# The merge with the tokens standing, and modulation weights in buffers of their own

## The chip, the cores and the metric

The kernel runs on one core of a Trainium2 chip. The metric is the device time of one execution in microseconds. Engines are called by their names or as the profile shortens them: TensorE (PE, its weight loads PEld), VectorE (DVE), ScalarE (ACT), GpSimd (POOL) and SyncE (SP), whose queue issues the DMAs in order.

## The reference: one layer of a hybrid diffusion backbone

256 tokens with 2048 channels pass one layer; 256 context tokens give keys, values and recurrence states besides. All is fp32.

```python
def modulate(x, w, shift, scale):
    return rms_norm(x, w) * (1.0 + scale) + shift

def merge_branches(att, rec, gate_a, gate_r, w_branch_attn, w_branch_rec, w_out):
    y = jax.nn.sigmoid(gate_a) * (att @ w_branch_attn) + jax.nn.sigmoid(gate_r) * (rec @ w_branch_rec)
    return y @ w_out

def hybrid_layer(...):
    sh1, sc1, g1, sh2, sc2, g2 = jnp.split(mod[:, None, :], N_MOD, axis=-1)
    h = modulate(x, norm1_w, sh1, sc1)
    hc = modulate(ctx, norm1_w, csh1, csc1)
    ak, av, rff, rfb, ri, aq, rq, rg, gate_a, gate_r = split_cols(h @ w_in, len(IN_SPLITS))
    ...
    att = diff_attn_readout(o_att, subln_w, lam_init)      # 8 heads, two softmaxes each, their difference
    rec = rec_readout(o_f + o_b, rg, rec_gnorm_w)          # 8 heads, gated linear recurrence both ways
    x = x + g1 * merge_branches(att, rec, gate_a, gate_r, w_branch_attn, w_branch_rec, w_out)
    x = x + g2 * conv_ffn(modulate(x, norm2_w, sh2, sc2), w_up, conv_w, conv_b, w_down)

def reference(...):
    mod = jax.nn.silu(c) @ w_mod[l] + b_mod[l]             # 2048 x 12288
    ...
    return rms_norm(x, final_norm_w)
```

## The kernel before

Activations lie with channels on the 128 partitions and tokens along the free axis, `hx[k]` holding 256 latent and 256 context tokens of channel block k. Every fp32 weight is split into a high part and a rest that TensorE multiplies in its faster fp32r form, and every activation likewise. `stage` (line 65) loads one 512 KB unit into the ring `raw` of four buffers, ScalarE casts it to `whi` (line 72), VectorE subtracts to get `wlo` (line 73), each with three buffers. A 128 x 128 block of weights stands in TensorE and tokens move. Where context is wanted, three 512-wide matmuls do a step (`mm3`, lines 77 to 79). For latent tokens alone, `gemm2_unit` (lines 126 and 127) uses a pair: `whi` against high and rest of x side by side (512 wide), `wlo` against the high part (256 wide); `fold` adds the two halves afterwards.

The stages follow each other: start-up (the first two of six modulation vectors, norm, first seven tiles), attention (8 heads), recurrence (8 heads), merge (16 channel blocks j: two gate tiles, a product with each branch, line 703 on; the gates are computed two j ahead), w_out, up product (44 pairs of tiles), down product (16 tiles of six units), final norm.

Beside the weights of the stages run "flows" (generators such as the steps of an attention head) and the modulation's remaining four vectors. `tick` is called once for every weight unit (twice for one of `mm3`), moves the flows on and calls `background` at a rate per stage (`BG_ATT`, `BG_REC`, `BG_MRG`). One background unit (line 336 on) loads 512 KB of w_mod into the same ring `raw`, and one unit later VectorE multiplies it with the conditioning vector `cb` and reduces it in one instruction (line 345). There are 128 such units, the last flushed in w_out at j = 10. `high_priority` in `stage` lets the scheduler put casts and splits ahead of other work of the two engines; otherwise the built order comes from the scheduler and the buffers.

Buffers of the tag `x1` (four of 4 KB a partition) hold first `cb`, then the recurrence's outputs `rraw`, gates, and the residual stream; those of the tag `ar` (16 of 2 KB) hold E and kn in the recurrence, att and rec, and later the normalized h2 of the up product. `acc` is three PSUM banks; `acc5` (tag `m`, four banks) lives from the merge on, in banks which the recurrence's pool `rps` had.

Two places of the recurrence matter below. At h = 0 the steps of head 0 (`ktp` line 565, `dc` 571, seven level products `lv` 590, `op` 598 to 601) stand beside gate tiles for j = 0 and 1 (line 655 in `pre`). Behind the last head come eight rg tiles, `drain`, and the statistic of the recurrence (lines 667 to 672), a Sqrt over all tokens.

## Time and profile before

| | |
|---|---|
| median of 3 runs | 1903.94 us (1903.0 to 1904.11) |
| the profiled execution | 1898.9 us |
| its span, first to last instruction | 1897.1 us |
| mean granted clock of TensorE | 0.996 of full speed |
| busy: TensorE, VectorE, ScalarE, GpSimd | 97%, 71%, 52%, 20% |
| moved by DMA | 385.71 MB, 203 GB/s over the span |

The stages in the profiled execution begin at about 0 (start-up), 145 (attention), 430 (recurrence), 800 (merge), 1057 (w_out), 1147 (up) and 1638 us (down). Times of instructions are from that one execution, so sums are to be held against its 1898.9 us, not against the median. "Idle before" an instruction is time its engine waited, with what released it. A matmul's start is recorded, its end is modelled: the distance from start to start tells what a stream of them costs.

### The profile page before, as it was taken

What the parts mean: (1) busy time and instruction counts of PE and PEld (TensorE: products, weight loads), DVE (VectorE), ACT (ScalarE), POOL (GpSimd) and SP (SyncE); (2) the same over time, 40 slices, a digit from 0 to 9 for tenths busy, and PEclk for the clock granted to TensorE, in tenths of its full rate; (3) what the DMA queues carried; (4) which work ended last, traced back from release to release, by engine and by line L of the source; (5) the groups of instructions that cost most, each with busy time, mean ns of one, the idle gap of its engine ahead of it and who ended that gap; (6) DMA issues with size and microseconds to landing.
All of it is one profiled execution on the core that took longest, in us unless ns stands there. A gap on an engine that the chain in (4) does not pass through costs nothing.

```text
span 1897.1 us, 27964 instructions
## 1 busy us (share of the span) xinstructions
PE 1841.9 (97%) x10430; PEld 1555.5 (82%) x10430; DVE 1354.3 (71%) x2130; ACT 992.7 (52%) x1501; POOL 377.6 (20%) x328
## 2 busy tenths in 40 slices
PE   7999999998999999999999999999999999999997
PEld 3777787777788888888888889888888888888886
DVE  4549878888866677977777879767677677654444
ACT  3336445447655556744444556555555555534442
POOL 0002111103223333401110110322222222211111
PEclk9999999999999999999999999999999999999998
DMA  9977665674333334688888865666666666666664
GB/s 374 370 274 248 202 197 186 207 267 145 97 111 113 110 103 122 210 269 273 280 272 272 276 192 183 192 189 190 190 188 191 188 195 187 185 193 187 192 192 123
DMA packets 112360, 385.71 MB, mean 203 GB/s; under 512 B 12384, under 2 KB 16608, under 8 KB 112224
## 3 DMA queue, kind: packets, MB, share of 16 engines
q1 hardware_dynamic: 112224, 383.92, 63.9%
q8 instruction: 82, 1.34, 0.3%
q14 instruction: 54, 0.44, 0.1%
HBM read 381.78 MB, written 2.10 MB: 202 GB/s over the span
## 4 chain that ended last, share of the span: by engine, by line
PE 72%; DMA 11%; DVE 10%; issue 4%; ACT 2%; POOL 0%; DVEq 0%; SPq 0%; ACTq 0%; POOLq 0%
PE macc L126 28%; PE macc L127 14%; DMA raw<-in_wm 8%; PE acc L126 5%; PE acc L78 4%; PE acc L79 4%; PE acc L77 4%; DVE wlo L73 3%; PE acc L127 3%; PE g L177 2%; DMA raw<-in_win 2%; DVE raw L345 2%; PE acc L177 2%; PE nat L177 2%; ACT whi L72 1%
## 5 line engine op out<-in xcount | busy, mean ns | idle before, releaser
L73 DVE TENSOR_TENSOR wlo<-raw,whi 128x1024 fp32r<-128x1024 f32 (+1 forms) x514 | 626.8, 1220 | 240.2 <-ACT whi L72 234.4
L72 ACT CAST whi<-raw 128x1024 fp32r<-128x1024 f32 (+1 forms) x514 | 530.6, 1033 | 469.9 <-PE macc L126 155.5
L126 PE MATMUL macc<-h,whi 128*128 128x512 f32 x1344 | 466.0, 391 | 0.0
L127 PE MATMUL macc<-h,wlo 128*128 128x256 f32 x1344 | 376.3, 280 | 0.0
L126 PE MATMUL acc<-h,whi 128*128 128x512 f32 x896 | 323.6, 402 | 1.1 <-DVE kkq L143 0.7
L126 PEld LDWEIGHTS macc<-h,whi 128*128 128x128 f32 x1344 | 251.3, 187 | 55.1
L127 PE MATMUL acc<-h,wlo 128*128 128x256 f32 x896 | 254.3, 284 | 6.2 <-DVE wlo L73 5.9
L127 PEld LDWEIGHTS macc<-h,wlo 128*128 128x128 f32 x1344 | 254.0, 189 | 0.0
L126 PE MATMUL macc<-f,whi 128*128 128x512 f32 x704 | 244.1, 391 | 0.0
L77 PE MATMUL acc<-h,whi 128*128 128x512 f32 x528 | 211.8, 401 | 0.0
L345 DVE SCALAR_TENSOR_TENSOR raw<-raw,cb 128x1024 f32<-128x1024 f32 x128 | 162.2, 1270 | 67.0 <-DMA raw<-in_wm 66.5
L78 PE MATMUL acc<-h,whi 128*128 128x512 f32 x528 | 207.0, 392 | 0.0
L79 PE MATMUL acc<-h,wlo 128*128 128x512 f32 x528 | 206.7, 391 | 0.0
L126 PEld LDWEIGHTS acc<-h,whi 128*128 128x128 f32 x896 | 169.1, 189 | 39.7 <-PE acc L127 1.0
L127 PE MATMUL macc<-f,wlo 128*128 128x256 f32 x704 | 197.1, 280 | 0.0
L127 PEld LDWEIGHTS acc<-h,wlo 128*128 128x128 f32 x896 | 170.0, 190 | 12.8 <-DVE wlo L73 12.2
L126 PEld LDWEIGHTS macc<-f,whi 128*128 128x128 f32 x704 | 131.6, 187 | 28.9
L842 POOL TENSOR_TENSOR u<-u 128x256 f32<-128x256 f32 x44 | 69.2, 1572 | 328.0 <-DVE u L837 288.0
L127 PEld LDWEIGHTS macc<-f,wlo 128*128 128x128 f32 x704 | 133.1, 189 | 0.0
L77 PEld LDWEIGHTS acc<-h,whi 128*128 128x128 f32 x528 | 99.2, 188 | 21.9 <-issue 2.9
L79 PEld LDWEIGHTS acc<-h,wlo 128*128 128x128 f32 x528 | 99.1, 188 | 21.5 <-issue 0.6
L78 PEld LDWEIGHTS acc<-h,whi 128*128 128x128 f32 x528 | 99.3, 188 | 20.5 <-issue 1.8
(740 smaller groups left out, 2639.0 us busy)
## 6 DMA issues: line engine op xcount, KB each, us to landing
raw<-in_win SPq DMA_DIRECT2D x178, 512.0 KB, 4.3
raw<-in_wup SPq DMA_DIRECT2D x168, 512.0 KB, 3.6
raw<-in_wm SPq DMA_DIRECT2D x128, 512.0 KB, 4.3
raw<-in_wdn SPq DMA_DIRECT2D x80, 512.0 KB, 3.7
nraw<-in_wn SPq DMA_DIRECT2D x64, 512.0 KB, 7.8
raw<-in_wout SPq DMA_DIRECT2D x32, 512.0 KB, 4.4
raw<-in_wba SPq DMA_DIRECT2D x16, 512.0 KB, 4.5
raw<-in_wbr SPq DMA_DIRECT2D x16, 512.0 KB, 4.7
```

The source lines that it names most:

```text
L72: act.copy(hi[:, :n], raw[:, :n])
L73: dve.tensor_sub(lo[:, :n], raw[:, :n], hi[:, :n].bitcast(F32))
L77: pe.matmul(ps, wh, xh, start=first, stop=False)
L78: pe.matmul(ps, wh, xl, start=False, stop=False)
L79: pe.matmul(ps, wl, xh, start=False, stop=last)
L126: pe.matmul(ps, hi[:, c_], xs[k][:, :, :T], start=k == 0, stop=False)
L127: pe.matmul(ps[:, :T], lo[:, c_], xs[k][:, 0, :T], start=False, stop=k == len(xs) - 1)
L177: tc.keep_in_program_order(pe.matmul(*args, **kw))
L345: dve.scalar_tensor_tensor(raw, raw, 1.0, cb[half], op0=ALU.mult, op1=ALU.mult, accum_out=modp[:, t - 32, half:half + 1])
L842: pool.tensor_tensor(cs[1], cs[0], cs[1], ALU.mult)
```

## The change

**Merge.** `gemmx` makes tokens stand and weights move: for a step of 128 input channels and 512 output channels, each half of the tokens takes three 512-wide matmuls (high x high, rest x high, high x rest), into two PSUM banks. Gate and branch weights are laid out 512 wide on the host (`wgt`, `wbr`). Four groups g of 512 channels replace sixteen j; results have tokens on partitions, so rrstd becomes a column of two values a partition, and the flow `turn` transposes each group back with eight transposes, through `acc` banks, into `y`. gate(0, 0) stands beside head 0 of the recurrence, gate(1, 0) behind the rg tiles, branch_att(0) behind `drain`. Head 0's flow starts its first step five ticks in, not one.

**Modulation.** `x1` has five buffers instead of four. In attention and merge a background unit takes an `x1` buffer, in the recurrence one of the ring as before (`lane`). Reductions wait in `held` until two ticks have passed. 96 units remain for these stages, half of them in the attention, all done before w_out, where sums and residual loads now stand. The last vector (16 tiles) is done as 64 half units of 256 KB in the down product, in `ar` buffers which the up product has released; the conditioning is loaded and computed again for it (`cond`, `cq`). Rates are set anew, NB is 9, the rg temporaries use the one buffer of the tag `sq`, and w_out takes four banks at a time.

```diff
-NB = 10
+NB = 9
-BG_ATT, BG_REC, BG_MRG = 0.7, 0.1, 0.55
+BG_ATT, BG_REC, BG_MRG, BG_DN = 0.63, 0.12, 0.46, 0.35
...
+    held = []
+
+    def background_end(age=0):
+
+        while held and held[0][0] >= age:
+            _, raw, c_, dst = held.pop(0)
+            dve.scalar_tensor_tensor(raw, raw, 1.0, c_, op0=ALU.mult, op1=ALU.mult, accum_out=dst)
 
     def tick(n):
         bg_rate[1] += n * bg_rate[0]
+        for item in held:
+            item[0] += n
+        background_end(2)
...
+    def gemmx(pss, units, xs, k=0):
+
+
+        for src in units:
+            hi, lo = stage(src, 1024)
+            for i in range(2):
+                c_ = slice(i * 512, (i + 1) * 512)
+                for m in range(2):
+                    t_ = slice(m * P, (m + 1) * P)
+                    pe.matmul(pss[m], xs[k][:, 0, t_], hi[:, c_], start=k == 0, stop=False)
+                    pe.matmul(pss[m], xs[k][:, 1, t_], hi[:, c_], start=False, stop=False)
+                for m in range(2):
+                    t_ = slice(m * P, (m + 1) * P)
+                    pe.matmul(pss[m], xs[k][:, 0, t_], lo[:, c_], start=False, stop=k == len(xs) - 1)
+                k += 1
+            tick(1)
...
+    def gate(i, g, accs):
+
+        pss = [accs() for _ in range(2)]
+        gemmx(pss, [wgt_d[i, g, u] for u in range(8)], hx)
+        dst = big.tile([P, 2, 512], F32, tag="x1", name="gate", bufs=5)
+        for m in range(2):
+            act.activation(dst[:, m], pss[m], AF.Sigmoid)
+        return dst
+
+    def branch_att(ga, g, accs):
+        pa = [accs() for _ in range(2)]
+        gemmx(pa, [wbr_d[0, g, u] for u in range(4)], att)
+        for m in range(2):
+            dve.tensor_mul(ga[:, m], pa[m], ga[:, m])
...
-                    raw = stg.tile([P, 1024], F32, tag="raw", name="raw", bufs=4)
+                    if lane[0]:
+                        raw = big.tile([P, 1024], F32, tag="x1", name="bgraw", bufs=5)
+                    else:
+                        raw = stg.tile([P, 1024], F32, tag="raw", name="raw", bufs=4)
                     dma.dma_start(raw, wm_d[t - 32, half])
...
-                yield 1
+                yield 5 if h == 0 else 1
...
-                    pre = [gates(j, g01[:, j]) for j in range(2)]
+                    pre = [gate(0, 0, acc3)]
...
-                t_ = rt.tile([P, T], F32, tag="rg", name="rg")
+                t_ = rt.tile([P, T], F32, tag="sq", name="rg")
...
+            pre.append(gate(1, 0, acc3))
             drain()
+
+            branch_att(pre[0], 0, acc3)
             sp = rps.tile([P, 4, P], F32, tag="aux", name="sp", bufs=2)
...
+            for m in range(2):
+                t_ = slice(m * P, (m + 1) * P)
+                pe.matmul(sp[:, m, 0:2], sqacc[:, t_], ones[:, 0:2], start=True, stop=False)
+                pe.matmul(sp[:, m, 0:2], sqlast[:, t_], ones[:, 0:2], start=False, stop=True)
+            act.activation(rrstd, sp[:, 0:2, 0], AF.Sqrt, bias=epst, scale=1.0 / 1024)
...
+    for g in range(4):
+        ga, gr = pre if g == 0 else [gate(i, g, acc5) for i in range(2)]
+        if g:
+            branch_att(ga, g, acc5)
+        pr = [acc5() for _ in range(2)]
+        gemmx(pr, [wbr_d[1, g, u] for u in range(4)], rec)
+        for m in range(2):
+            dve.scalar_tensor_tensor(gr[:, m], pr[m], rrstd[:, m:m + 1], gr[:, m], op0=ALU.mult, op1=ALU.mult)
+            dve.tensor_add(gr[:, m], gr[:, m], ga[:, m])
+        yy = et.tile([P, 4, 2, T], F32R, tag="y", name=f"y{g}", bufs=4)
+        start(turn(yy, gr))
+        y += [yy[:, i] for i in range(4)]
+    background(len(bg))
+    background_end()
...
+    cq = [big.tile([P, 512], F32, tag="ar", name=f"cq{i}", bufs=16) for i in range(4)]
+    cond(cq, big.tile([P, 512], F32, tag="ar", name="sg", bufs=16), lambda ins: ins)
...
+                raw = big.tile([P, 512], F32, tag="ar", name="bgraw", bufs=16)
+                dma.dma_start(raw, wm_d[48 + t, q // 2, :, (q % 2) * 512:(q % 2 + 1) * 512])
+                held.append([0, raw, cq[q], modq[:, t, q:q + 1]])
+
+    bgf[0] = background_last
+    bg_rate[:] = 2 * BG_DN, 0.0
+    background_last(8)
```

VectorE in the merge, before. `wlo` is the split of a weight unit, line 345 the reduction of a modulation unit, `t` and `gate` the folds and products of a block.

```order
L345 SCALAR_TENSOR_TENSOR raw,modp<-raw,cb_81 128x1024
L73 TENSOR_TENSOR wlo<-raw,whi 128x1024
L143 TENSOR_TENSOR gate<-gate,acc 128x256
L345 SCALAR_TENSOR_TENSOR raw,modp<-raw,cb_81 128x1024
L73 TENSOR_TENSOR wlo<-raw,whi 128x1024 x2
L143 TENSOR_TENSOR gate<-gate,acc 128x256
```

The same engine in the merge, after, in group 1; the reduction is now line 93.

```order
L73 TENSOR_TENSOR wlo_7507<-raw_7504,whi_7506 128x1024
L93 SCALAR_TENSOR_TENSOR bgraw_7502,modp_78<-bgraw_7502,cb1_82 128x1024
L93 SCALAR_TENSOR_TENSOR bgraw_7541,modp_78<-bgraw_7541,cb1_82 128x1024
L73 TENSOR_TENSOR wlo_7525<-raw_7522,whi_7524 128x1024
L73 TENSOR_TENSOR wlo_7546<-raw_7543,whi_7545 128x1024
L93 SCALAR_TENSOR_TENSOR bgraw_7580,modp_78<-bgraw_7580,cb1_82 128x1024
```

The reductions read buffers of their own (`bgraw`), in pairs, and the folds between the splits are gone.

TensorE at the level products of head 0 (`lv`, from the E tiles that ScalarE and VectorE make), before; `acc` is a tile of w_in's product beside it.

```order
L77 MATMUL acc_4129<-h13_1089,whi_4175 128x512
L590 MATMUL lv_3989<-E_3924 128x128 x2
L590 MATMUL lv_4022<-E_3957 128x128 x2
L590 MATMUL lv_4064<-E_3994 128x128 x2
L590 MATMUL lv_4097<-E_4027 128x128 x2
L78 MATMUL acc_4129<-h13_1089,whi_4175 128x512
```

And after, the last of them:

```order
L78 MATMUL acc_3996<-h15_1211,whi_4052 128x512
L79 MATMUL acc_3996<-h15_1211,wlo_4053 128x512
L632 MATMUL lv_4080<-E_4033 128x128 x2
L632 MATMUL lv_4091<-E_4044 128x128 x2
L77 MATMUL acc_4103<-h0_247,whi_4106 128x512
```

Before, four levels stand in a row; now two, with products of the input projection ahead and behind.

VectorE where the down product begins, before; `wlo_15514` is the fifth unit of the first down tile, `wlo_15536` its sixth.

```order
L73 TENSOR_TENSOR wlo_15492<-raw_15489,whi_15491 128x1024
L843 TENSOR_TENSOR sg_15413<-sg_15413,u_15409 128x256
L73 TENSOR_TENSOR wlo_15514<-raw_15511,whi_15513 128x1024
L73 TENSOR_TENSOR wlo_15536<-raw_15533,whi_15535 128x512
L73 TENSOR_TENSOR wlo_15555<-raw_15552,whi_15554 128x1024
```

And after, where `wlo_14828` is the fifth unit and `wlo_14853` the sixth:

```order
L73 TENSOR_TENSOR wlo_14828<-raw_14825,whi_14827 128x1024
L186 TENSOR_TENSOR cq3_14692<-cq3_14692,sg_14693 128x512
L93 SCALAR_TENSOR_TENSOR bgraw_14709,modq_79<-bgraw_14709,cq1_14690 128x512
L93 SCALAR_TENSOR_TENSOR bgraw_14711,modq_79<-bgraw_14711,cq2_14691 128x512
L93 SCALAR_TENSOR_TENSOR bgraw_14713,modq_79<-bgraw_14713,cq3_14692 128x512
L93 SCALAR_TENSOR_TENSOR bgraw_14715,modq_79<-bgraw_14715,cq0_14689 128x512
L93 SCALAR_TENSOR_TENSOR bgraw_14717,modq_79<-bgraw_14717,cq1_14690 128x512
L93 SCALAR_TENSOR_TENSOR bgraw_14719,modq_79<-bgraw_14719,cq2_14691 128x512
L93 SCALAR_TENSOR_TENSOR bgraw_14721,modq_79<-bgraw_14721,cq3_14692 128x512
L93 SCALAR_TENSOR_TENSOR bgraw_14776,modq_79<-bgraw_14776,cq0_14689 128x512
L73 TENSOR_TENSOR wlo_14853<-raw_14850,whi_14852 128x512
```

Nine operations of the last modulation vector stand between the two splits that followed each other.

## Rows read from the trace of the kernel before

**Rows 1.** The page: busy time of the engines; the chain that ended last.
```profile
PE 1841.9 (97%) x10430; PEld 1555.5 (82%) x10430; DVE 1354.3 (71%) x2130; ACT 992.7 (52%) x1501; POOL 377.6 (20%) x328
...
PE 72%; DMA 11%; DVE 10%; issue 4%; ACT 2%; POOL 0%; DVEq 0%; SPq 0%; ACTq 0%; POOLq 0%
PE macc L126 28%; PE macc L127 14%; DMA raw<-in_wm 8%; PE acc L126 5%; PE acc L78 4%; PE acc L79 4%; PE acc L77 4%; DVE wlo L73 3%; PE acc L127 3%; PE g L177 2%; DMA raw<-in_win 2%; DVE raw L345 2%; PE acc L177 2%; PE nat L177 2%; ACT whi L72 1%
```

**Rows 2.** Stretches: length, PE, PEld, DVE, ACT, POOL busy (instructions); clock, DMA share, GB/s.
```profile
145.00:320.00 175.00, 168.85 (x842) 135.46 (x841) 148.89 (x255) 89.38 (x154) 28.73 (x25) 0.99 0.66 210
320.00:440.00 120.00, 113.01 (x584) 92.67 (x583) 97.65 (x163) 62.30 (x104) 8.85 (x13) 1.00 0.71 228
440.00:500.00 60.00, 51.79 (x278) 42.67 (x277) 55.67 (x99) 43.62 (x62) 23.00 (x23) 1.00 0.34 106
...
780.00:800.00 20.00, 18.18 (x104) 15.54 (x104) 19.38 (x39) 14.11 (x27) 5.28 (x4) 1.00 0.78 257
800.00:1057.00 257.00, 251.31 (x1393) 212.87 (x1392) 197.55 (x282) 119.67 (x188) 29.73 (x31) 1.00 0.84 274
...
1638.00:1885.00 247.00, 245.33 (x1414) 215.66 (x1412) 120.29 (x132) 99.81 (x115) 37.53 (x32) 1.00 0.61 177
```

**Rows 3.** Timeline of TensorE: start us, us, what; three places.
```profile
210.09 0.39 PE L79 MATMUL acc<-h,wlo 128*128 128x512 f32 x1
...
211.00 0.39 PE L77 MATMUL acc<-h,whi 128*128 128x512 f32 x1
...
258.39 0.60 PE L425 MATMUL tp<-ident,vr 128*128 128x128 f32 x4
...
259.06 0.28 PE L127 MATMUL acc<-h,wlo 128*128 128x256 f32 x1
...
797.73 0.40 PE L126 MATMUL acc<-h,whi 128*128 128x512 f32 x1
...
802.68 0.40 PE L126 MATMUL acc<-h,whi 128*128 128x512 f32 x1
```

**Rows 4.** Waits in the merge, 780 or 800 to 1057: total us, times, longest.
```profile
PE acc L127 <- DVE wlo L73: 5.1, 12, 1.0
...
SPq L341 <- DVE raw L345: 67.9, 34, 3.7
...
DVE raw L345 <- DMA raw<-in_wm: 32.8, 36, 2.5
```

**Rows 5.** The page's DMA issues: KB each, median us from issue to landing.
```profile
raw<-in_wm SPq DMA_DIRECT2D x128, 512.0 KB, 4.3
```

**Rows 6.** Waits of TensorE from 440 to 500 us.
```profile
PE ktp L565 <- DVE KQ L526: 2.8, 1, 2.8
...
PE lv L590 <- DVE E L552: 1.0, 2, 0.6
```

**Rows 7.** Timeline of ScalarE at the end of the recurrence.
```profile
797.73 1.28 ACT L671 ACT_TABLE_LOAD   x1
799.02 0.48 ACT L671 ACTIVATE rrstd<-sp,epst 128x256 f32<-128x256 f32 x1
```

**Rows 8.** Waits of TensorE in the attention, 145 to 440 us.
```profile
PE S L395 <- ACT p L402: 8.2, 7, 2.2
...
PE acc L127 <- DVE wlo L73: 0.8, 1, 0.8
```

**Rows 9.** Waits of SyncE's queue and of VectorE from 145 to 320 us.
```profile
SPq L68 <- DVE raw L345: 27.9, 13, 4.4
...
DVE raw L345 <- DMA raw<-in_wm: 12.1, 7, 4.5
DVE wlo L73 <- ACT whi L72: 8.1, 6, 3.1
```

**Rows 10.** VectorE by line and shape: busy us, mean ns; idle before, releaser.
```profile
L345 DVE SCALAR_TENSOR_TENSOR raw<-raw,cb 128x1024 f32<-128x1024 f32 x128 | 162.2, 1270 | 67.0 <-DMA raw<-in_wm 66.5
...
L408 DVE SCALAR_TENSOR_TENSOR p<-p,z 128x512 f32<-128x512 f32 x16 | 11.9, 745 | 0.0
```

More of the change, by code (lines that the diff above doesn't have):

```diff
@@ L146, in body, with cond @@
     modv = cpool.tile([P, 96], F32, name="modv")
-    modp = cpool.tile([P, 64, 2], F32, name="modp")
+    modp = cpool.tile([P, 48, 2], F32, name="modp")
+    modq = cpool.tile([P, 16, 4], F32, name="modq")
     sel = cpool.tile([P, 2], F32, name="sel")
-    cb = [big.tile([P, 1024], F32, tag="x1", name=f"cb{i}", bufs=4) for i in range(2)]
+    cb = [big.tile([P, 1024], F32, tag="x1", name=f"cb{i}", bufs=5) for i in range(2)]
+    def cond(parts, sg, pin):
+        n = D // len(parts)
+        for i, part in enumerate(parts):
+            dma.dma_start(part, cb_d[:, i * n:(i + 1) * n])
+            pin(act.activation(sg, part, AF.Sigmoid))
+            pin(dve.tensor_mul(part, part, sg))
     hx = [None] * KT
@@ L294, in body @@
             g0raw[GROUP0[i]] = r
-        sg = big.tile([P, 1024], F32, tag="x1", name="sg", bufs=4)
-        for i in range(2):
-            dma.dma_start(cb[i], cb_d[:, i * 1024:(i + 1) * 1024])
-            tc.keep_in_program_order(act.activation(sg, cb[i], AF.Sigmoid))
-            tc.keep_in_program_order(dve.tensor_mul(cb[i], cb[i], sg))
+        cond(cb, big.tile([P, 1024], F32, tag="x1", name="sg", bufs=5), tc.keep_in_program_order)
     def in_units(t):
@@ L320, in in_tile_early, with acc3 @@
         g0raw[t] = r
-    def gates(j, dst):
-        for i, base in enumerate((GA, GR)):
-            ps = in_tile(base + j)
-            fold(dst[:, i], ps)
-            act.activation(dst[:, i], dst[:, i], AF.Sigmoid)
-        return [dst[:, 0], dst[:, 1]]
-    bg = [(t, half) for half in range(2) for t in range(32, 96)]
+    def acc3():
+        return acc.tile([P, 512], F32, tag="acc", name="acc")
+    def gate(i, g, accs):
[10 more added lines that the diff above has]
+            dve.tensor_mul(ga[:, m], pa[m], ga[:, m])
+    bg = [(t, half) for half in range(2) for t in range(32, 80)]
     with ExitStack() as esa:
-        bg_rate[0] = BG_ATT
-        held = []
+        bg_rate[0] = BG_ATT0
+        lane = [True]
         def background(n):
@@ L483, in body @@
             drain()
-        rraw = [big.tile([P, 4, T], F32, tag="x1", name=f"rraw{i}", bufs=4) for i in range(2)]
-        rrstd = cpool.tile([P, T], F32, name="rrstd")
+        rraw = [big.tile([P, 4, T], F32, tag="x1", name=f"rraw{i}", bufs=5) for i in range(2)]
+        rrstd = cpool.tile([P, 2], F32, name="rrstd")
         with ExitStack() as es:
@@ L611, in head @@
                     pool.tensor_tensor(sqacc, sqacc, sq, ALU.add)
-            background(max(0, len(bg) - 64))
-            g01 = big.tile([P, 2, 2, T], F32, tag="x1", name="g01", bufs=4)
+            background(max(0, len(bg) - 48))
+            background_end()
+            lane[0] = False
             depth[0] = 1
@@ L690, in residual_load @@
     def residual_load(i):
-        t_ = big.tile([P, 4, T], F32, tag="x1", name=f"x1_{i}", bufs=4)
+        t_ = big.tile([P, 4, T], F32, tag="x1", name=f"x1_{i}", bufs=5)
         dma.dma_start(t_, xT_d[:, 4 * i:4 * i + 4])
@@ L725, in body @@
+    background(len(bg))
+    background_end()
+    bg_rate[0] = 0.0
+    mod_sum(32, 80)
+    w2 = cpool.tile([P, KT], F32, name="w2")
+    dve.scalar_tensor_tensor(w2, modv[:, 64:80], 1.0, col("n2w", 0, 16), op0=ALU.add, op1=ALU.mult)
+    for i in range(4):
+        residual_load(i)
     warm = et.tile([P, 1], F32, name="warm")
@@ L767, in body @@
     for j in range(KT):
-        if j % 2 == 0:
-            pair = [(acc5(), [(wout_d[j + i, 0], 1024), (wout_d[j + i, 1], 1024)]) for i in range(2)]
+        if j % 4 == 0:
+            four = [(acc5(), [(wout_d[j + i, 0], 1024), (wout_d[j + i, 1], 1024)]) for i in range(4)]
             if j == 0:
-                gemm2(pair, y)
-        if j > 1:
-            gemm2([pair[j % 2]], y)
-        ps = pair[j % 2][0]
-        sq = residual(j, ps, 32, sqs)
-        if j == 10:
-            background(1000)
-            residual_load(3)
-            mod_sum(48, 96)
-            w2 = cpool.tile([P, KT], F32, name="w2")
-            dve.scalar_tensor_tensor(w2, modv[:, 64:80], 1.0, col("n2w", 0, 16), op0=ALU.add, op1=ALU.mult)
+                gemm2(four, y)
+                drain()
+        if j > 3:
+            gemm2([four[j % 4]], y)
+        ps = four[j % 4][0]
+        sq = residual(j, ps, 32, sqs)
         if j >= 10:
@@ L848, in body @@
         else:
-            fj = et.tile([P, 2, T], F32R, tag="y", name=f"f{j}", bufs=16)
+            if j % 4 == 0:
+                fp = et.tile([P, 4, 2, T], F32R, tag="y", name=f"f{j}", bufs=4)
+            fj = fp[:, j % 4]
         act.copy(fj[:, 0], sg)
```

82 lines of the change are left out of this document (37 added, 45 removed).

## The prediction

> **What bounds the kernel now.** I read the page's busy line and chain first: TensorE is busy 97% of the span, and the chain that ended last is 72% TensorE, 11% DMA, 10% VectorE, the largest DMA piece being `raw<-in_wm`, the modulation weights [rows 1]. So time can leave in two ways: TensorE does less, or its remaining waits get shorter. The table by stretch says where those waits are [rows 2]. The down product (1638 to 1885) holds 1414 matmuls, 707 pairs of a 512-wide and a 256-wide one, in 247 us: 349 ns a pair, with VectorE busy under half the time. That is the stage without stalls. The attention (two rows, 145 to 440) is idle 6.2 and 7.0 us, the start of the recurrence (440 to 500) 8.2 us, its last 20 us 1.8 us, the merge (800 to 1057) 5.7 us. In the merge idle time shows only part of the loss: a late matmul is recorded as a long one, so I go by the pitch.
>
> The pitch from start to start [rows 3]: four 512-wide matmuls from 210.09 to 211.00 us, 0.2275 each. In the merge's gates 14 pairs from 797.73 to 802.68, 353.6 ns a pair. Four transposes with the slow matmul behind them, 258.39 to 259.06 us, less an ordinary 0.235: 0.435 us, 109 ns each.
>
> **The merge's matmuls.** The change computes gates and branches with the tokens standing. Before: 32 gate tiles x 16 = 512 pairs at 353.6 ns (181.0 us) and 32 branch tiles x 8 = 256 pairs at 349 ns, the down product's row, since these too read x without a gap (89.4): 270.4 us. After: 8 gate passes of 16 steps and 8 branch passes of 8 make 192 steps of six 512-wide matmuls, 1152 x 0.2275 = 262.1 us, and 32 transposes x 0.109 = 3.5 us. Net **-4.8 us**. All of it is on the path, as TensorE is the bound. (The folds go too, but VectorE and ScalarE work beside TensorE.) The bound on the other side is pairs at 349 throughout, the lowest pitch shown: 268.0 against 265.6, -2.4.
>
> The Trainium skill speaks against this gain: "TensorE: Matmul & The Clock Gate", Back-to-back issue gap, gives an isolated gap of N/2.4 + 2.5 ns, 216 and 109 ns, and by it eight matmuls (4 x 216 + 4 x 109 = 1300 ns) cost what six do (1296), so that only the transposes would be left, +2.7 us, and the whole sum 7.5 us later. The rows disagree: 228 ns instead of 216, and 350 or more a pair instead of 325; I go by the rows.
>
> **The merge's stalls.** Between 800 and 1057 us lie 1393 matmuls, 448 gate pairs and some 248 branch pairs: 158.4 + 86.8 = 245.2 us at their pitch, so 11.8 us are stalls. The waits tell why [rows 4]: TensorE waits for the low half of the weights (`wlo`); SyncE, issuing in order, stands 67.9 us, 34 times, ahead of a modulation load that waits for a buffer which VectorE has to free by its reduction, and weight loads stand behind; VectorE waits 32.8 us for the modulation data to land, with `wlo` splits queued behind. One ring of four buffers carries both streams. A load lands 4.3 us after its issue (median) [rows 5]; a unit lasts 8 x 0.35 = 2.8 us, and at 0.55 modulation units a tick four buffers are 2.6 weight units, 7.2 us of lead, of which the splits take part. After, the weights own the ring (4 x 2.73 = 10.9 us), the modulation has buffers of its own, and the built order stands reductions at least two units behind their loads. DMA stays the same size, some 192 GB/s of weights and 0.46 units a tick more, about 280 GB/s, what the row of the stretch shows (274 at a share of 0.84). I leave 2 us of stalls: **-9.8 us**, with 0 and -11.8 as bounds.
>
> **Start of the recurrence.** The 8.2 us of idle time are shared [rows 6]: the first `ktp` waits 2.8 us for VectorE's KQ, then level products of head 0 wait for E, and shorter waits follow. In the changed order the first `ktp` has the same cover since head 0's q product (135 and 138 512-wide matmuls, by my count of the order), so its 2.8 us mostly stay, though VectorE and ScalarE lose the folds of four gate tiles. Behind it the levels get 78 matmuls of cover where 45 stood: the row of four level products without anything between is gone. I take **-5 us** (the short waits, and small gaps that the idle time doesn't count), with 0 and -8.2 as bounds.
>
> **End of the recurrence.** gate(1,0) and branch_att(0), 96 + 48 matmuls, move in front of the end, so they cover `op` of head 7. But the four small matmuls for rrstd are followed directly by a product into a PSUM bank which the recurrence's own banks cover, and it waits for the Sqrt that reads them: in the rows of before a cast of some 1 us may stand ahead, then a table load of 1.28 us, then the Sqrt of 0.48 [rows 7]; some 2.3 us of TensorE. Also the rg temporaries now share one buffer, so eight folds wait for POOL one after the other. Against that stands the 1.8 us idle in 780 to 800. I take **0**, from -2 to +4. The Trainium skill puts a drain of about 1.38 us beside each table load ("ScalarE: Activation LUTs", What ACT_TABLE_LOAD costs); here the Sqrt starts 1.29 us after its load did, so no run shows one in this place, and it would add to the end of my range alone.
>
> **Attention.** Modulation loads leave the weights' ring here too. SyncE waited 27.9 us in 13 times with a weight load for a modulation buffer [rows 9]. But the new buffers are free earlier, and the order packs 48 reductions before the 32nd weight unit where 36 stood: 12 x 1.27 us [rows 10] = 15.2 us more for VectorE, which in 145 to 320 is busy 148.9 of 175. None follow until the recurrence, where before 28 did: some 35 us less in the second part. TensorE waits there mainly for the softmax (`S` for `p`, 8.2 us in 7 times [rows 8]), whose steps stand in VectorE's queue. I expect the second part to give back half of its 7.0 us idle and the first to stay: **-3 us**. Bounds: -10 (three quarters of all 13.2 us) and +8 (VectorE's 164 busy plus its present waits for data and for casts, 12.1 and 8.1 [rows 9], exceed 175 by 9).
>
> **Up to down.** The last gate's 64 half units, in the h2 buffers, start when the up product releases these. SyncE issues 4 conditioning loads and 11 half units, each waiting for TensorE, in front of the sixth load of the first down tile; VectorE does one product and eight 512-wide reductions between the fifth and sixth `wlo`, 9 x 0.8 us (a 512-wide operation of the same kind took 745 ns [rows 10], with an accumulator read) = 7.2 us. Three split buffers give a split two units, 5.6 us, less about 2.4 for cast and split, 3.2 us of slack: a stall of 7.2 - 3.2 = **+4 us**, from 0 (it was cast early) to +8 (DMA late as well). Later tiles: four reductions add 3.3 us to some 7.5 of VectorE's 15.4 a tile; no stall.
>
> **Nothing** for w_out with four banks (covered by its own 349 ns pairs), NB = 9 (start-up loads; if that cover fails up to +3), or the residual loads, which now go out before w_out.
>
> Sum against the profiled run, 1898.9 us: -4.8 - 9.8 - 5 + 0 - 3 + 4 = -18.6, 1880.3. The median of the three runs is 1903.94, 5.0 above it, so I add 5.0: **1885.3**, say 1885.
>
> **The rivals.** (A) More comes free: attention gives 10 instead of 3, and the end of the recurrence its 2: 1876, or down to 1869 with the start at its bound. For it: VectorE is what these waits end on, and it loses work there. Against: one S bank stays. (B) The first part of the attention becomes VectorE's: +8 instead of -3 and the later parts as forecast, 1896; with the landing waits of 12 us unmoved up to 1905, near no change. For it: 94% busy. (C) The merge's stalls are the DMA's rate, not the shared ring: share 0.84 before, the same bytes after; then 1885 + 9.8 = 1895. Against it: SyncE's and VectorE's waits name the buffer. The change would then do what it says and be worth half. (D) Slower: in-order SyncE in the attention. Three of the five buffers are free for modulation loads (the conditioning keeps two), and every load behind a busy one holds the weight loads back. 48 units in 170 us is one per 3.5 us, so a buffer's round must stay under 10.6 us: 4.3 to land, 1.3 to reduce, 5.0 in VectorE's queue. If rounds take 13 us, 16 of them are 38 us late, and the weights' lead, four units of some 5 us less landing, cast and split, absorbs about 13: +25, 1910. It decides from a queue wait of some 7 us. Before, SyncE already waited, at most 4.4 us at a time on these [rows 9], yet TensorE lost 0.8 us to `wlo` [rows 8]; so a small chance.
>
> **How the numbers follow.** Forecast (1874 to 1897) 0.58, A 0.14, B 0.10, C 0.10, D 0.08. A measurement of this kernel can tell about 0.2%, 3.8 us, from no change, so "same" is 1900.1 to 1907.7. Faster: 0.57 of the forecast, A, 0.02 to 0.03 of B, most of C, less a reserve for what I haven't seen: 0.79. Same: the upper part of B and a little of C and D: 0.10. Slower: D and the reserve: 0.11. The range leaves out the lower edge of A and D with the top of B: 1869 to 1901.
>
> **What would show it.** Right: merge passes at 0.2275 us a matmul with nearly no `acc <- wlo` waits, SyncE's wait for modulation buffers gone from weight loads; no `lv` waits at head 0; a TensorE gap near 2 us before the first rec product and near 4 us in the first down tile. Wrong: `wlo` waits in the merge at a DMA share near 0.85 (C), VectorE over 95% busy and `wlo` waits in 145 to 320 (B), SyncE waiting long for `bgraw` there (D), or the granted clock at its 1.2 GHz level behind one of the new gaps.

## The result: slower, by 0.7%

The changed kernel takes 1915.24 us (median of 4 runs, 1914.17 to 1917.5) against 1903.47 us before: a ratio of 1.0067 (95% interval 1.0054 to 1.0080). The forecast of 1885 us and its range of 1869 to 1901 us are missed on the wrong side of no change. Two executions taken beside the experiments, one of e1 at 6478 us and one of the kernel before at 4767 us, are left out of every median and ratio below.

The profiled execution has a span of 1915.7 us against 1897.1, 18.6 us more than before (the medians differ by 11.8). Here are the page's busy line and the head of its chain, which answer to [rows 1].

```profile
PE 1844.7 (96%) x10082; PEld 1548.3 (81%) x10082; DVE 1345.9 (70%) x2148; ACT 982.5 (51%) x1423; POOL 342.5 (18%) x296
...
PE 74%; DVE 14%; ACT 4%; issue 3%; DMA 3%; POOL 2%; SPq 0%; DVEq 0%; ACTq 0%; POOLq 0%
```

TensorE has 348 matmuls fewer and is busy for 3 us longer. On the chain DMA fell from 11% to 3%, as meant, while VectorE rose from 10% to 14%, and TensorE, ScalarE and GpSimd by 2 points each: what DMA gave up, the engines took.

To see where, I added up from the starts of all matmuls in the trace how far each lies behind the one ahead of it, less what its shape costs in an undisturbed stream (227, 117 and 112 ns for 512, 256 and 128 columns), and counted what is over 60 ns. In that loss both waits and a slow clock are contained. Times are those of each kernel's own trace; "e" columns are experiments below.

| stretch, us | before | after | e1 | e3 | e5 | e8 |
|---|---|---|---|---|---|---|
| 160 to 440, attention | 28.0 | 19.9 | 19.9 | 29.4 | 29.5 | 19.4 |
| 440 to 520, heads 0 and 1 | 12.6 | 16.9 | 17.9 | 16.1 | 14.3 | 17.9 |
| 520 to 760, later heads | 8.6 | 21.2 | 7.8 | 21.8 | 21.8 | 7.4 |
| 760 to 840, end of recurrence | 5.1 | 6.8 | 9.7 | 8.4 | 11.5 | 4.0 |
| 840 to 1080, merge | 13.8 | 7.6 | 2.7 | 6.0 | 13.9 | 2.6 |
| 1600 to 1880, down product | 0 | 14.6 | 15.7 | 19.1 | 0 | 0 |
| whole execution | 104.5 | 123.1 | 110.4 | 137.1 | 132.4 | 89.9 |

So the change did what the forecast hoped for in the attention (8 us) and the merge (6 us), and lost 17 us in the recurrence and 15 in the down product, besides 2 at the recurrence's end. The whole rows differ by 18.6 us, as the spans do; savings and losses under 60 ns a matmul (the merge has fewer, w_out and the down product a slower stream, see e9) cancel.

The stretches, to be read as [rows 2] (length; PE, PEld, DVE, ACT, POOL busy and instructions; clock, DMA share, GB/s):

```profile
145.00:320.00 175.00, 167.34 (x843) 134.18 (x843) 162.12 (x282) 88.57 (x156) 28.49 (x24) 1.00 0.71 242
320.00:440.00 120.00, 119.79 (x599) 98.41 (x598) 75.83 (x120) 68.26 (x104) 9.10 (x13) 1.00 0.41 126
...
520.00:760.00 240.00, 229.43 (x1186) 195.74 (x1185) 166.69 (x308) 135.97 (x184) 71.26 (x71) 0.99 0.34 105
...
1640.00:1880.00 240.00, 229.59 (x1288) 197.86 (x1287) 157.93 (x283) 94.38 (x109) 39.74 (x29) 0.99 0.78 248
```

The second part of the attention is idle for 0.2 us of 120 where it was 7.0. Between 520 and 760 us TensorE is now idle for 10.6 us; before, the same row had none:

```profile
520.00:760.00 240.00, 240.00 (x1255) 205.49 (x1254) 170.17 (x322) 138.59 (x194) 78.55 (x76) 1.00 0.37 112
```

**The recurrence.** TensorE's waits from 440 to 820 us in the changed kernel (total, times, longest), which answer to [rows 6]:

```profile
PE lv L632 <- DVE E L594: 15.1, 5, 6.9
PE ktp L607 <- issue: 2.7, 1, 2.7
PE lv L632 <- DVE S L635: 1.9, 1, 1.9
```

VectorE around one of the five, in order of start (start, duration), and the matmul that waited for it:

```profile
551.41 0.43 DVE L593 TENSOR_TENSOR E<-E,kkq 128x256 f32<-128x256 f32 x1 [0.72 <-ACT E L591]
551.75 0.69 DVE L686 TENSOR_TENSOR_SCAN PL<-ones,fq 128x256 f32<-128x256 f32 x1
552.35 1.22 DVE L73 TENSOR_TENSOR wlo<-raw,whi 128x1024 fp32r<-128x1024 f32 x1
553.49 1.26 DVE L686 TENSOR_TENSOR_SCAN PL<-ones,fq 128x256 f32<-128x256 f32 x2
554.67 1.25 DVE L688 TENSOR_TENSOR_SCAN PC<-ones,fq 128x256 f32<-128x256 f32 x2
555.84 0.88 DVE L635 COPY_PREDICATED S<-masks,lv 128x128 f32<-128x128 uint32 x4
556.62 0.42 DVE L594 TENSOR_TENSOR E<-E,kkq 128x256 f32<-128x256 f32 x1
...
557.18 0.68 PE L632 MATMUL lv<-E 128*128 128x128 f32 x4 [2.10 <-DVE E L594]
```

A level's E is multiplied in two halves. The first (line 593) starts at 551.4 us; the second (line 594) stands behind the next head's five scans, a split and four masked copies, and starts 5.2 us later. The level product needs both. Counted in the trace by the order of the level products, the five waits stand one each at heads 1, 2, 4, 5 and 6, and the 1.9 us for `S` at head 3. Head 0 has none, where before it had three of up to 1.0 us.

**The down product.** Waits of TensorE and of VectorE from 1640 to 1880 us:

```profile
PE macc L137 <- DVE wlo L73: 10.4, 10, 2.3
...
DVE bgraw L93 <- DMA bgraw<-in_wm: 23.6, 16, 3.7
```

The timeline of VectorE in one such place (start, duration; idle before, releaser):

```profile
1753.27 1.22 DVE L73 TENSOR_TENSOR wlo<-raw,whi 128x1024 fp32r<-128x1024 f32 x1
1758.16 0.69 DVE L93 SCALAR_TENSOR_TENSOR bgraw<-bgraw,cq 128x512 f32<-128x512 f32 x1 [3.67 <-DMA bgraw<-in_wm]
1758.78 0.08 DVE L93 DVE_READ_ACCUMULATOR bgraw<-bgraw,cq 128x1 f32 x1
1758.90 0.16 DVE L931 TENSOR_REDUCE modv<-modq 128x1 f32<-128x4 f32 x1
1758.97 0.68 DVE L93 SCALAR_TENSOR_TENSOR bgraw<-bgraw,cq 128x512 f32<-128x512 f32 x1
1759.58 0.08 DVE L93 DVE_READ_ACCUMULATOR bgraw<-bgraw,cq 128x1 f32 x1
1759.58 1.22 DVE L73 TENSOR_TENSOR wlo<-raw,whi 128x1024 fp32r<-128x1024 f32 x1
```

VectorE stands for 3.7 us at the head of its queue with a reduction whose half unit has not landed; the split that TensorE needs comes behind two reductions. By the trace the reductions stand in the first nine tiles, 12, 6 and 5 in the first three, 8 in each of the next five and 1 in the ninth, where the rate in the code says four a tile.

**The clock.** It differs too. In stretches of 3.4 us TensorE ran at the lower of its two levels, 1.2 GHz: once in mid-kernel before (226.7 us), six times after, one of them 6.8 us long. Three of them (the last column but two is the clock as a share of full speed):

```profile
447.60:451.00 3.40, 3.40 (x16) 3.30 (x16) 2.77 (x8) 1.62 (x2) 0.14 (x1) 0.50 0.18 74
502.20:509.00 6.80, 3.94 (x16) 3.69 (x16) 6.20 (x13) 2.21 (x4) 3.94 (x5) 0.50 0.09 38
...
1761.70:1765.10 3.40, 3.40 (x13) 2.92 (x12) 3.40 (x7) 0.42 (x2) 1.11 (x2) 0.50 0.75 215
```

Each of the six lies behind or partly within a wait of TensorE (of the three shown: 2.7 us for `ktp`, 6.9 for `lv`, 2.3 for the split). Together they are 23.9 us at half speed against 3.4 before, so up to 10 of the 18.6 us (half of the 20.5 us more) are this second price of the waits. The prediction priced none of its waits with it.

### The profile page after: what moved, and what is told of

Read it like the earlier page. It is cut to its first block, busy times and chain, and to the rows that moved or that the text cites. A ratio compares the mean times of both kernels' runs of the same rounds, so it can differ in the third digit from the quotient of the medians.

```text
span 1915.7 us, 27159 instructions
## 1 busy us (share of the span) xinstructions
PE 1844.7 (96%) x10082; PEld 1548.3 (81%) x10082; DVE 1345.9 (70%) x2148; ACT 982.5 (51%) x1423; POOL 342.5 (18%) x296
## 4 chain that ended last, share of the span: by engine, by line
PE 74%; DVE 14%; ACT 4%; issue 3%; DMA 3%; POOL 2%; SPq 0%; DVEq 0%; ACTq 0%; POOLq 0%
PE macc L136 24%; PE macc L137 13%; DVE wlo L73 4%; PE macc L160 4%; PE macc L161 4%; PE macc L164 4%; PE acc L77 3%; PE acc L78 3%; PE acc L79 3%; DVE bgraw L93 3%; PE acc L136 3%; DMA bgraw<-in_wm 2%; PE g L214 2%; PE acc L214 2%; PE nat L214 2%
## 5 line engine op out<-in xcount | busy, mean ns | idle before, releaser
L136 PE MATMUL macc<-f,whi 128*128 128x512 f32 x704 | 248.9, 398 | 0.0
L77 PE MATMUL acc<-h,whi 128*128 128x512 f32 x528 | 212.1, 402 | 0.0
L78 PE MATMUL acc<-h,whi 128*128 128x512 f32 x528 | 206.7, 391 | 0.0
L136 PE MATMUL acc<-h,whi 128*128 128x512 f32 x384 | 141.8, 409 | 0.0
L799 POOL TENSOR_TENSOR sqs<-sqs,sq 128x256 f32<-128x256 f32 x28 | 34.0, 1216 | 507.0 <-ACT sq L798 507.0
L77 PEld LDWEIGHTS acc<-h,whi 128*128 128x128 f32 x528 | 99.7, 189 | 23.4 <-issue 4.6
L79 PEld LDWEIGHTS acc<-h,wlo 128*128 128x128 f32 x528 | 99.3, 188 | 21.0
L78 PEld LDWEIGHTS acc<-h,whi 128*128 128x128 f32 x528 | 99.5, 188 | 18.7 <-issue 0.4
L137 PE MATMUL acc<-h,wlo 128*128 128x256 f32 x384 | 108.5, 283 | 0.0
L93 DVE SCALAR_TENSOR_TENSOR bgraw<-bgraw,cb 128x1024 f32<-128x1024 f32 x81 | 98.9, 1230 | 11.2 <-DMA bgraw<-in_wm 11.2
L136 PE MATMUL macc<-y,whi 128*128 128x512 f32 x256 | 90.7, 399 | 0.0
```

The costliest lines, as they stand in the source:

```text
L77: pe.matmul(ps, wh, xh, start=first, stop=False)
L78: pe.matmul(ps, wh, xl, start=False, stop=False)
L79: pe.matmul(ps, wl, xh, start=False, stop=last)
L93: dve.scalar_tensor_tensor(raw, raw, 1.0, c_, op0=ALU.mult, op1=ALU.mult, accum_out=dst)
L136: pe.matmul(ps, hi[:, c_], xs[k][:, :, :T], start=k == 0, stop=False)
L137: pe.matmul(ps[:, :T], lo[:, c_], xs[k][:, 0, :T], start=False, stop=k == len(xs) - 1)
```

## The experiments

My theory (A) after this reading: the 5 ticks moved every head against the next head's gate arithmetic; in the down product VectorE stands with reductions for late data; buffers of their own helped attention and merge. The rivals are in each expectation.

### e1: the 5 ticks put back to 1

```diff
-                yield 5 if h == 0 else 1
+                yield 1
```

> The changed kernel with one number put back: head 0 of the recurrence takes its first step after 1 tick, not 5. Theory A: the 5 ticks shift every head's steps against the next head's gate arithmetic, so that VectorE's E product of a level stands behind a split, five scans and four masked copies; TensorE's loss beyond its pitch between 440 and 760 us is 38 us in the changed kernel against 21 before. Then this run loses the 2.1 us lv waits of each head and gains 12 to 17 us: 1898 to 1903. Rival: the loss comes with gate(0,0), whose 512-wide results and sigmoids stand beside head 0, or from the modulation; then the lv waits stay and the time stays near 1915.

Measured: 1903.37 us (median of nine runs), 1.0010 of before (0.9997 to 1.0022), 11.9 us less than the changed kernel's median. Between 520 and 760 us no wait of TensorE is left:

```profile
520.00:760.00 240.00, 240.00 (x1263) 205.85 (x1262) 170.66 (x327) 135.77 (x187) 84.81 (x76) 1.00 0.38 118
```

The loss there falls from 21.2 to 7.8 us. The gain lies at the lower edge of the 12 to 17 us expected; in this trace the end of the recurrence loses 2.9 us more. The first heads stay bad (17.9 us): that is not the ticks.

### e5: the 5 ticks alone, in the kernel before

```diff
-                yield 1
+                yield 5 if h == 0 else 1
```

> The kernel before with one number of the change alone: head 0 of the recurrence takes its first step after 5 ticks instead of 1. Theory A: this alone makes each later head lose some 2 us at a level product; TensorE's loss between 520 and 760 us rises from 8.6 to about 20 us, the clock falls in one or two more places, and the kernel is 8 to 15 us slower than before, 1.004 to 1.008 of it. Rival: the 5 ticks only hurt together with gate(0,0) and the new modulation lanes; then it is within 0.2% of before.

Measured: 1921.49 us, 1.0102 of before (1.0079 to 1.0125), 18.8 us slower. One number, without the new merge or a new buffer, costs more than the whole change does, and more than the 8 to 15 us expected. Of what this trace loses more than before, 13 us lie in the later heads, 6 at the end of the recurrence and 5 in w_out, behind a wait of 2.4 us for `y`. The waits of TensorE from 520 to 760 us in this kernel:

```profile
PE lv L590 <- DVE E L552: 9.8, 4, 3.0
```

Before, the same row had no wait. It is the wait of the changed kernel, for the same second half (line 552 here). The rival, that it hurts only beside gate(0,0), falls.

### e2: no last modulation vector in the down product

```diff
-    bgl = [(t, q) for t in range(16) for q in range(4)]
+    bgl = []
+    dve.memset(modq, 0.0)
```

> The changed kernel without the loads and reductions of the last modulation vector in the down product (that vector is left out of the result, its sums are zero). Theory A: these cost the down product 14.6 us of TensorE time beyond its pitch, so 1915 falls to about 1899 to 1901 and every down tile takes 15.25 us. Rival: the slower pitch of the later down tiles (15.55 us instead of 15.25) and the longer down product come from elsewhere (the up product's new buffers, the clock); then less than 8 us return.

Measured: 1899.41 us, 0.9985 of before (0.9973 to 0.9996), 15.8 us less than the changed kernel. The down product is as before, without a wait:

```profile
1640.00:1880.00 240.00, 240.00 (x1387) 211.63 (x1386) 120.03 (x131) 99.69 (x115) 37.27 (x31) 1.00 0.62 182
```

1387 matmuls in 240 us, where the changed kernel did 1288.

### e4: the 64 reductions without their loads

```diff
-                raw = big.tile([P, 512], F32, tag="ar", name="bgraw", bufs=16)
-                dma.dma_start(raw, wm_d[48 + t, q // 2, :, (q % 2) * 512:(q % 2 + 1) * 512])
-                held.append([0, raw, cq[q], modq[:, t, q:q + 1]])
+                held.append([0, one[0], one[1], modq[:, t, q:q + 1]])
```

> The changed kernel with the 64 reductions of the last vector in the down product, on two constant tiles, without their 64 loads (the last vector is wrong). Theory A: TensorE's stalls there come from reductions that wait for late loads at the head of VectorE's in-order queue, splits behind them; without loads under 4 us of stalls remain of 14.6: about 1903. Rival: VectorE's added work by itself makes the splits late; then the stalls stay, 1911 to 1917, since here up to eleven reductions stand in a tile.

Measured: 1899.97 us, 0.9990 of before (0.9976 to 1.0004), 0.6 us from the run without the vector. Waits of TensorE in the down product, and the row of that stretch:

```profile
PE macc L137 <- DVE wlo L73: 0.9, 3, 0.5
```

```profile
1640.00:1880.00 240.00, 239.00 (x1368) 208.88 (x1368) 162.12 (x285) 97.64 (x112) 38.60 (x31) 1.00 0.61 180
```

VectorE is as busy as in the changed kernel (162 against 158 us of 240) and TensorE hardly waits. So it is not VectorE's work but its standing still for data, or the loads by some other way; the next run bears on which.

### e6: the loads at their planned rate

DMA issues of the down product are kept in program order from the second tile on.

```diff
+        if j == 1:
+            pin[0] = tc.keep_in_program_order
...
-        dma.dma_start(raw[:, :n], src)
+        pin[0](dma.dma_start(raw[:, :n], src))
...
-                dma.dma_start(raw, wm_d[48 + t, q // 2, :, (q % 2) * 512:(q % 2 + 1) * 512])
+                pin[0](dma.dma_start(raw, wm_d[48 + t, q // 2, :, (q % 2) * 512:(q % 2 + 1) * 512]))
```

> The changed kernel with the DMA issues of the down product kept in program order from its second tile on, so that the half units of the last vector come at the planned rate, 4 a tile over 13 tiles, not 7 to 8 a tile in the first nine; same loads, same reductions. Theory A: the late landings behind which VectorE stands come from two streams that together ask for 295 GB/s; spread out (some 255 GB/s) most of the 10 us behind the first tile return, the first tile's 4 us stay: 1904 to 1908. Rival: a reduction right behind its load waits whatever the rate; then 1912 to 1917.

Measured: 1912.49 us, 1.0054 of before (1.0037 to 1.0070): 2.8 us better than the changed kernel, not the 7 to 11 expected. My theory's figure falls, the rival's holds. The waits in the down product:

```profile
DVE bgraw L95 <- DMA bgraw<-in_wm: 56.8, 34, 4.4
...
PE macc L139 <- DVE wlo L75: 9.8, 9, 2.6
```

From the third tile on four or five units are reduced a tile, where the changed kernel has up to eight, yet VectorE waits longer (56.8 us, 34 times) and TensorE as long. Behind the first two tiles, which lose 3.0 us more here, this run loses 8.5 us, the changed kernel 10.7. So the rate of the two streams explains little: a reduction that the built order puts shortly behind its load waits for the landing at either rate, and the split behind it is late. No run holds the reductions back longer, which would test this directly.

### e3: the modulation in the weights' ring again

```diff
-                    if lane[0]:
+                    if False:
```

> The changed kernel with the modulation units of all stages in the ring of the weights, as before; the new merge, the last vector in the down product and the 5 ticks stay. Theory A: buffers of their own gave the merge 6 us and the attention 8 us back, so this run is 10 to 14 us slower than the changed kernel, 1925 to 1929, with splits late in the merge. Rival: the tokens standing (no folds, fewer loads of standing operands) gave them, and the ring matters little: 1913 to 1918.

Measured: 1925.35 us, 1.0114 of before (1.0089 to 1.0138), some 10 us slower than the changed kernel, as expected. But the place is not as expected: the attention loses all that it had gained (29.4 us against 19.9, before 28.0), the down product 4.5 more, and the merge nothing (6.0 against 7.6). SyncE does wait in the merge of this run for the shared buffers, with weight loads behind it, and TensorE's splits are in time. From 840 to 1056 us:

```profile
PE macc L164 <- DVE wlo L73: 0.4, 1, 0.4
...
SPq L387 <- DVE raw L93: 42.3, 18, 3.5
SPq L68 <- DVE raw L93: 30.6, 14, 4.7
```

So it is not the ring by itself that the merge's stalls of before went with. What else changed there is the new product, which spares folds (VectorE is busy 143 us of 214 in this run's merge against 166 of 216 before), and the modulation's lower rate: 32 reductions stand in this run's merge, 41 in those 216 us before, at a DMA share of 0.79 against 0.85. Which of these it was, no run separates, and so rival C's cause, the rate of DMA, isn't excluded for the stalls of before.

### e7: 5 ticks to 1, the last vector in the up product

32 whole units, in buffers of the tag `h` which are free there, at 0.4 a tick from tile 4 of the up product on.

```diff
-                yield 5 if h == 0 else 1
+                yield 1
...
+        if j == 4:
+            cq = [big.tile([P, 1024], F32, tag="h", name=f"cq{i}", bufs=16) for i in range(2)]
+            cond(cq, big.tile([P, 1024], F32, tag="h", name="sg", bufs=16), lambda ins: ins)
+            bgf[0] = background_last
+            bg_rate[:] = BG_UP, 0.0
```

> The changed kernel with 1 tick instead of 5 at head 0, and the last modulation vector as 32 whole units in the up product, in buffers of its h tag that are free there, instead of the down product. Theory A: up has no stalls, DMA at 190 GB/s and VectorE at 73%, so it hides 32 units at 0.4 a tick; both losses are gone and the gains stay: 1885 to 1892, faster than before. Rival: the up product takes over the stalls (VectorE above 85% there, loads late), 1897 or more.

Measured: 1899.49 us, 0.9965 of before (0.9940 to 0.9990), but ten runs in two groups: three from 1885.0 to 1888.6, seven from 1898.6 to 1902.1. The three lie in the expected range, the seven where the rival put them, but the stalls of the rival are absent: in the profiled execution, one of the seven, TensorE waits for a split once, 0.4 us. Neither the expectation nor its rival has two groups.

### e8: the same, with rg's own buffer

```diff
-                t_ = rt.tile([P, T], F32, tag="sq", name="rg")
+                t_ = rt.tile([P, T], F32, tag="rg", name="rg")
```

> As the run with the last vector in the up product, with the rg temporaries in a buffer of their own again instead of the shared one of the tag sq. Theory A: the waits of TensorE for rg's fold (3.5 us in the run with 1 tick) go: 2 to 4 us faster than that run. Rival: another wait of the end of the recurrence takes their place, no difference.

Measured: 1894.32 us (five runs, 1892.1 to 1895.2), 0.9955 of before (0.9940 to 0.9970). The end of the recurrence loses 4.0 us where e1 lost 9.7 (e7, without the buffer, 9.5), somewhat more than the expected 2 to 4 us: in e1's trace the waits for rg's fold are 3.5 us with a slow stretch of the clock behind them (792.6 us), and in e8's both are absent. This is a reading of traces; the times alone can't show it, given e7's two groups. TensorE's whole loss is 89.9 us, 14.6 under before, yet the profiled span is only 7.0 under it.

### e9: a different stream of matmuls in between

So 7.6 us are missing in e8, and some 12 if the merge's matmuls spare the 4.8 us forecast. They are mainly in the pitch. In the up and down products of e8, nearly without waits, a pair takes 353 ns, where before it took 347. Does an interruption change it back?

```diff
+    def stir(w, x):
+        d_ = acc.tile([P, 512], F32, tag="acc", name="stir")
+        for i in range(12):
+            pe.matmul(d_[:, :T], w[:, 0, :P], x[:, 0, :T], start=i == 0, stop=i == 11)
...
+        if j in (24, 32):
+            stir(h2[0], h2[1])
...
+    stir(ff[0], ff[1])
```

> The kernel with the last vector in up and its own rg buffer, plus three groups of twelve 256-wide matmuls into a bank that nobody reads: two in the up product (tiles 24 and 32), one ahead of the down product. Theory M: pairs of matmuls run at one of two steady pitches, 347 or 353 ns, and an interruption of the stream decides which; in that kernel up and down run at 353 from 1247 us on. If a different stream of matmuls is such an interruption, the pitch falls back to 347 behind one of the groups, and the 4.2 us that they cost are repaid with up to 10: 1886 to 1890. Rival: the pitch follows from where operands or results lie in memory; then it stays 353, and the time is 4 us longer, 1898.

Measured: 1897.83 us, 0.9976 of before (0.9964 to 0.9987). The pitch stays at 353 behind all three groups, and the groups themselves run at 120 ns a matmul, not 117. A different stream is no interruption in this sense. The time is what the rival expected; its reason, the place of operands and results, doesn't fit e11 below, where the same program holds the other pitch.

### e10 and e11: the same without the last vector, and e8 once more

e10 has 1 tick, rg's own buffer, and the edit of e2; against e8 it lacks the last vector. e11 is the kernel of e8, unchanged.

```diff
-    bgl = [(t, q) for t in range(16) for q in range(4)]
+    bgl = []
+    dve.memset(modq, 0.0)
```

> The changed kernel with 1 tick at head 0, rg in its own buffer, and no last modulation vector at all (its sums are zero and the result lacks it). It differs from the run with the last vector in up by those 32 units alone. Theory M: the units there cost no wait (TensorE lost 1 us beyond its pitch in that up product) but put the stream of up and down on the 353 ns pitch; without them both stay at 347, which for 1376 pairs from 1247 us on and the down product's 704 is 12 us less: about 1880 to 1884. Rival: the slow pitch comes from the new layout or from the chip; then up and down stay at 353 here too, and the time is 1892 to 1895.

> The kernel with the last vector in the up product and rg in its own buffer once more, on this chip beside the run without the last vector. If the pitch is a state that an execution falls into and not a property of the program, its executions spread over some 12 us (1882 to 1896), as they did with the shared rg buffer (1885 to 1902); if it is a property of the program, they lie within 4 us of 1894.

Measured: e10 takes 1882.40 us (1880.5 to 1884.1), 0.9889 of before (0.9869 to 0.9908). e11's ten runs spread from 1879.6 to 1898.2 us with a median of 1894.01, 0.9935 of before (0.9912 to 0.9957). Its profiled execution, of 1879.6 us, has a span of 1877.6 us against 1890.1 in e8, and the same program's loss is the same: 89.5 and 89.9 us. Forty microseconds of the up product, in the kernel before, in e8, in e11 and in e10, as rows of stretches:

```profile
1240.00:1280.00 40.00, 40.00 (x233) 35.28 (x232) 28.64 (x41) 22.72 (x36) 11.63 (x8) 1.00 0.64 192
```

```profile
1240.00:1280.00 40.00, 40.00 (x229) 34.71 (x228) 35.05 (x53) 23.71 (x38) 10.08 (x7) 1.00 0.78 277
```

```profile
1240.00:1280.00 40.00, 40.00 (x233) 35.18 (x232) 35.01 (x54) 24.28 (x38) 9.39 (x7) 1.00 0.79 275
```

```profile
1240.00:1280.00 40.00, 40.00 (x233) 35.27 (x232) 27.98 (x40) 24.06 (x38) 10.67 (x8) 1.00 0.59 186
```

233, 229, 233 and 233 matmuls in 40 us without an idle moment, at the same granted clock and, in e8 and e11, with the same instructions. So the pitch is a state that an execution falls into. The two traces come from different chips, but the ten runs of e11, on one chip, spread over 18.6 us, so the chip alone doesn't decide it. e10's four runs without the units lie close together, and its trace holds 347 ns through up and down; the trace of e11 shows that the units don't force 353. Whether they make it likelier is open. With 12.5 us the pitch is as large as the effect of the whole change.

At the pitch of before, e11's span is 19.5 us under before and its loss 15.0: the other 4.5 us are close to the 4.8 that the merge's matmuls were forecast to spare.

## Why the prediction was wrong, point by point

**The step that failed first** was in "Start of the recurrence". It costed the 5 ticks by the cover they give to head 0, where I read two kernels' orders, and the seven heads behind it at nothing. Flows run one after the other there, so a delay of the first moves them all, and what a head's steps meet in VectorE's queue changes with it. Expected -5 us for the stage; measured +4.3 in heads 0 and 1, +12.6 in the later ones, and by itself, in the kernel before, 18.8 us (e5). At head 0 the sign came as forecast, no `lv` waits: the mechanism held where I looked and failed in the heads behind. In the trace of the changed kernel the pattern repeats with each head.

The row of 2.8 us in [rows 6] I also read for the wrong head. It belongs to head 1; head 0's `ktp`, the first, waited 1.9 us:

```profile
453.59 0.63 PE L565 MATMUL ktp<-ident,KQ 128*128 128x128 f32 x4 [1.87 <-issue]
...
487.44 0.66 PE L565 MATMUL ktp<-ident,KQ 128*128 128x128 f32 x4 [2.76 <-DVE KQ L526]
```

That the first `ktp` of the changed kernel waits 2.7 us, near the 2.8 I left there, is luck; head 1's has no wait any more.

**The term that was mis-sized** is "Up to down", +4 us with a bound of +8; it cost 14.6 us beyond the pitch, 15.8 by e2. The first two tiles were as forecast (3.9 us). Its "no stall" for the later tiles was wrong by its reckoning: it compared VectorE's work with the time of a tile and left out that a reduction waits for its data at the head of an in-order queue. e4 shows that the work alone costs little (2.3 us of loss there). I also took four units a tile from the rate in the code; the run has up to eight, twelve in the first. e6 shows that four would have helped little.

**Rival D** had nearly this mechanism, in-order issue and late modulation data, and put it in the attention and on SyncE. There, from 145 to 320 us, VectorE now waits 0.2 us for such data where it was 12.1 [rows 9], and SyncE's waits for a modulation buffer are at most 4.0 us long; TensorE waits for no split in the attention:

```profile
DVE bgraw L93 <- DMA bgraw<-in_wm: 0.2, 1, 0.2
...
SPq L387 <- DVE bgraw L93: 54.0, 31, 4.0
```

**Right number, wrong reason: the merge.** -9.8 us for the stalls; they fell by 6.2 in the changed kernel and by 11.1 in e1, where one wait and a slow stretch of the clock are absent. But e3 shows that the shared ring alone wasn't the cause, though the waits of [rows 4] named it, and leaves the cause open between the new product and the modulation's lower rate. Nor did DMA stay the same size in the merge, as the prediction had it: its share fell from 0.85 to 0.76. A named wait of a queue is no stall of TensorE until TensorE waits too. The matmuls of the first term came as forecast: the changed kernel's 1152 have a median distance of 227 ns, and e11 above shows about their gain. (The 349 ns a pair taken for the branches is a row with 1.7 us of idle time in it; the pairs of that stage run at 347.)

**The attention** gave 8.1 us, inside the bounds of -10 to +8 and more than the 3 chosen; e3 shows that this is the work of the separate buffers. With them 48 reductions stand in the first part and 2 in the second, in e3 34 and 16; whether this packing gave the gain, as the forecast had it, or the ring left to the weights, no run separates. The second part gave back 6.8 of its 7.0 us of idle time where half was forecast, and the first has 1.5 us more. (By its own sum the upper bound was 9, not 8; nothing hung on it.) Rival B (VectorE too busy in the first part) is refuted: VectorE is busy 162 of 175 us there, as B reckoned, without B's cost.

**The end of the recurrence**: TensorE waits 1.5 us for the Sqrt of rrstd (forecast some 2.3), on a stage that lost 1.7 us more, within -2 to +4. The shared rg buffer costs some 5.5 us beside 1 tick (e1 and e7 against e8), more than the +4 that I allowed for the whole stage. By the trace the Sqrt starts 1.30 us after its table load, as it did before, and no drain shows between them.

```profile
837.88 1.28 ACT L718 ACT_TABLE_LOAD   x1
839.18 0.26 ACT L718 ACTIVATE rrstd<-sp,epst 128x2 f32<-128x2 f32 x1
...
839.49 0.50 PE L160 MATMUL macc<-whi,rec 128*128 128x512 f32 x1 [1.47 <-ACT rrstd L718]
```

**Left out of the sum** were the two surcharges on a wait: the granted clock behind it (named as a sign only, without a price; 20.5 us more at 1.2 GHz than before), and the pitch.

What stays open: why heads 0 and 1 lose 14 to 20 us in every version with gate(0,0) beside them, and what puts TensorE on one pitch or the other. For the first the traces name waits and no common cause: 6.9 us for E at head 1 in the changed kernel, 4.6 us for KQ at head 1 in e1 and e8.

The best version measured that computes the whole layer is e8, at 1894 us in two series (0.9955 and 0.9935 of before); with the pitch of 347 ns in up and down the one execution seen took 1879.6.

## What to carry to other kernels

When a flow of steps shares an in-order engine with the next round's arithmetic, the phase between them is a cost term of its own: read the built order through one whole round, not only where the edit stands. Work that is moved into a stage with a half idle engine is free only if its data have landed when its turn comes; reckon the wait at the head of the queue, and prefer a stage where the loads can run far ahead. And a wait named for a queue must be followed to the bounding engine before it is priced.

## What the runs showed of the hardware

- TensorE's stream of fp32r pairs has two steady pitches at the full granted clock: 347 ns (230 + 117) and 353.6 ns (236 + 117). An execution can hold either through 700 us, and the same program was seen in both (1877.6 and 1890.1 us of span, on two chips; ten runs on one of these spread over 18.6 us). In the changed kernel the down product begins at 347, goes over to 353 within its stalls and stays there: its last tiles take 15.55 us instead of 15.25. In e1 it is at 353 in the third tile and ends at 347 (15.25).
- Waits of 1.5 to 6.9 us on TensorE were followed in six places by 3.4 or 6.8 us at 1.2 GHz; waits of 1.9 to 2.1 us at 555, 603, 651 and 700 us were not, nor the 2.8 us at 485 us in the kernel before. A wait's length alone doesn't tell.
